# Weight operands prepared for fast multiplications: stores one operand behind, raw quarters two ahead, plain quarters not stored

## The chip, the core and the metric

The kernel runs on one core of a Trainium2 chip. Its time is the device time of one execution in microseconds. TensorE (PE) multiplies, ScalarE (ACT), VectorE (DVE) and GpSimd (POOL) work on rows, SyncE (SP) issues the DMAs spoken of here. Every engine runs its own instructions in order.

## The reference

One layer of an encoder, 1024 tokens of width 1024, in float32:

```
h   = rms_norm(x);  lru_in, gate, q, k, v, g_r, g_a = split(h @ W_in)
y_r = (gelu(gate) * rg_lru(conv4(lru_in))) @ W_lru_o
y_a = diff_attention(rms_norm(q), rms_norm(k), v) @ W_attn_o
x   = x + (sigmoid(g_r) * y_r + sigmoid(g_a) * y_a) @ W_out
x   = x + memory_cross_attention(rms_norm(x), rms_norm(mem))
x   = x + experts(rms_norm(x))        # 32 experts, two per token
```

The change is about the three products with W_attn_o (`w_ao`), W_lru_o (`w_lo`) and W_out (`w_out`).

## The kernel before

Every float32 operand is split in two parts: `h`, a rounded copy made by ScalarE, and `l`, the rest, made by VectorE (`split`, L323 to L325; for weights that stream in, L97 and L101). A product is three matmuls, hh, hl and lh (`mm3`, L158 to L161). All big tiles are slots of 128 x 1024 of one pool with 51 of them; a tile that is allocated waits until the last reader of the slot it gets is done, a DMA included.

The stages, in the profiled execution's time:

- 0 to 86 us: x is loaded, normed and transposed.
- to 357 us: the projections v (first half), q and k (four units, `qk_steps`), v (second half). One unit has four quarters, `pqk<unit>_<quarter>` or `pv<unit>_<quarter>`, each 48 matmuls into a two-bank tile of which there are two. After a quarter ScalarE empties its bank twice: `sq` (L350, squares) and `tm` (L351, a copy); then VectorE sums (L353), GpSimd forms the root (L224, L225), VectorE scales `tm` (L356), and GpSimd rotates a part of it (L361 to L364). TensorE transposes `tm` into `pT<unit>_<quarter>_<i>` (L374), ScalarE evicts that to `qk` (L375).
- Between the matmuls of this stage `prepare` (L438) works for later: each of the three products above is done with 7 instead of 8 block multiplications (1024 x 1024 in quarters, sums and differences of quarters being the operands). For each weight and each half `lp` it loads four raw quarters `qw_*` (L431), forms the seven operands with additions on VectorE (L411), splits each into `phw_*` on ScalarE and `plw_*` on VectorE, and stores both in DRAM, in `pre_d` (L454, L455). The raw quarters of the next weight half are loaded when operand 5 is emitted. `tm_proj` advances it by `PRE[0]` steps after each half quarter.
- 357 to 870 us: attention and gates; to 966 us: the recurrence.
- 966.70 to 1197 us: the three fast multiplications (`multiply`), 21 products `g` of 10.9 us, seven for each weight: w_ao first, w_lo from g = 7 at 1043, w_out from g = 14 at 1119.13 us. `preloaded` loads the stored operands back two products ahead, `computed` forms and splits those of the activations (`op<n><p><lp>h`, `l`, L914 to L924) one product ahead.
- to 1300 us: attention to the memory and the router; to 1964 us: the experts, whose weights stream in by DMA.

The order of the instructions on an engine comes from a list scheduler in the compiler, which places them by priority and by its own estimate of times; the code's order is the priority. Loads of `prepare` and `preloaded` carry an extra dependence on the last matmul that the code had issued (`W.after(d, W.last)`), the stores none.

Of the kernel before, what the change touches and what calls it, by code (L numbers as in the profile page):

```python
# [12 lines left out]
F32R = mybir.dt.float32r  # L13
BF = mybir.dt.bfloat16
I32 = mybir.dt.int32
AF = mybir.ActivationFunctionType
OP = mybir.AluOpType
# [27 lines left out]
class Weights:  # L45
# [20 lines left out]
    def load(self):  # L66
        while self.loaded < min(len(self.pieces), self.split + self.load_ahead):
            i = self.loaded
            t = self.pool.tile([P, 1024], F32, tag="s", name=f"wraw{i}")
            src = self.pieces[i]  # L70
            j = min(i - self.load_ahead, self.split - 1)
            if len(src.shape) == 2:
                todo = [(t, src)]
            else:
                to = t.rearrange("p (k h c) -> p k h c", k=2, h=2)
                todo = [(to[:, k], src[k]) for k in range(2)]
            for to, src in todo:
                d = self.nc.sync.dma_start(to, src)
                if j >= 0:
                    self.after(d, self.h_ins[j])  # L80
                if self.floor is not None:
                    self.after(d, self.floor)
            self.dma.append(d)
            if self.flying and i >= self.flying:
                self.after(d, self.dma[i - self.flying], sync=True)
            self.raw[i] = t
            self.loaded += 1
# [44 lines left out]
def block_kernel(ctx, tc, a):  # L132
    nc = tc.nc
# [10 lines left out]
    V, A, G, E = nc.vector, nc.scalar, nc.gpsimd, nc.tensor  # L144

    def slot(name, dt=F32, shape=(P, 1024)):
        return S.tile(list(shape), dt, tag="s", name=name)

    def bank(name, dt=F32, shape=(P, 512)):
        return pb1.tile(list(shape), dt, tag="b1", name=name)  # L150

    def bank2(name, dt=F32, shape=(P, 1024)):
        return pb2.tile(list(shape), dt, tag="b2", name=name)

    def f(x):
        return x.bitcast(F32)
# [37 lines left out]
    W = Weights(nc, tc, S, pieces)  # L194
# [3 lines left out]
    for tb in range(NB):  # L198
        t = slot(f"x{tb}")
# [76 lines left out]
    for i in range(8):  # L276
        G.memset(frq[:, i:i + 1], INV_FREQ[i])
    V.tensor_tensor(ang, posf[:, :, None].to_broadcast([P, NB, 8]), frq[:, None, :].to_broadcast([P, NB, 8]),
                    op=OP.mult)
# [43 lines left out]
    def split(src, h, l):  # L323
        A.activation(h, src, AF.Copy)  # L324
        V.tensor_tensor(l, src, f(h), op=OP.subtract)  # L325
# [99 lines left out]
    def half(t, i, lp):  # L425
        return t[4 * (i // 2) + 2 * lp:4 * (i // 2) + 2 * lp + 2, :, (i % 2) * 512:(i % 2) * 512 + 512].rearrange(
            "h p c -> p h c")

    def quarter(name, src):
        t = slot(name)  # L430
        d = nc.sync.dma_start(t.rearrange("p (h c) -> p h c", h=2) if len(src.shape) == 3 else t, src)  # L431
        if W.last is not None:
            W.after(d, W.last)
        return t

    pre_d = {n: dp.tile([7, 2, 2, P, 1024], F32, name=f"pre_{n}") for n in ("w_ao", "w_lo", "w_out")}

    def prepare():  # L438

        units = [(n, lp) for n in pre_d for lp in range(2)]  # L440

        def load(n, lp):
            return {i: [quarter(f"q{n}{lp}{i}", a[n][i % 2, 2 * (i // 2) + lp] if n == "w_out" else half(a[n], i, lp))]
                    for i in range(4)}

        q = load(*units[0])
        yield
        for u, (n, lp) in enumerate(units):
            nxt = []

            def emit(p, tiles):
                h, l = slot(f"ph{n}{lp}{p}", F32R), slot(f"pl{n}{lp}{p}", F32R)
                split(tiles[0], h, l)
                nc.sync.dma_start(pre_d[n][p, lp, 0], f(h))  # L454
                nc.sync.dma_start(pre_d[n][p, lp, 1], f(l))  # L455
                if p == 5 and u + 1 < len(units):
                    nxt.append(load(*units[u + 1]))

            yield from operand_steps(q, n == "w_out", emit)
            q = nxt[0] if nxt else None  # L460

    pre = prepare()
    W.split_ahead = 4
    first = v_steps(0)
# [432 lines left out]
    stages, ops = [], {}  # L897
    QUARTER = {1: 0, 4: 2, 5: 3, 6: 1}

    def preloaded(name):  # L900
        while True:
            for p in range(7):
                r = []
                for lp in range(2):
                    t = [slot(f"{name}{p}{lp}{x}", F32R) for x in "hl"]
                    for i in range(2):
                        d = nc.sync.dma_start(f(t[i]), pre_d[name][p, lp, i])
                        W.after(d, W.last)
                    r.append(t)
                yield r  # L910

    def computed(q, moving, scale=None):
        done = []

        def emit(p, tiles):
            r = []
            for lp, t in enumerate(tiles):
                h, l = slot(f"op{len(ops)}{p}{lp}h", F32R), slot(f"op{len(ops)}{p}{lp}l", F32R)
                if scale is None:
                    W.after(A.activation(h, t, AF.Copy), W.last)  # L920
                    V.tensor_tensor(l, t, f(h), op=OP.subtract)
                else:
                    W.after(A.activation(h, t, AF.Copy, scale=scale), W.last)
                    V.scalar_tensor_tensor(l, t, scale, f(h), op0=OP.mult, op1=OP.subtract)  # L924
                r.append((h, l))
            done.append(r)

        steps = operand_steps(q, moving, emit)
        for _ in range(7):
            while not done:  # L930
                next(steps)
            yield done.pop()

    def lane_out(t, blk, k):
        return [x[:, (blk % 2) * 512 + k * P:(blk % 2) * 512 + k * P + P] for x in t[blk // 2]]
# [4 lines left out]
    def operands(g, side):  # L940
        if g // 7 < len(stages):
            ops[g, side] = next(stages[g // 7][side])

    def multiply(n, before, out):
        lane = stages[n][2]
        p1, u2, u3 = [None] * 2, [None] * 2, [None] * 2
        for p in range(7):
            g = 7 * n + p
            ta, tb_ = ops.pop((g, 0)), ops.pop((g, 1))
            for blk in range(4):  # L950
                lp, c = blk // 2, slice((blk % 2) * 512, (blk % 2) * 512 + 512)
                if g % 2 == 0:
                    if blk % 2 == 0:
                        both = bank2(f"pw{n}_{p}_{blk}")
                    ps = both[:, c]
                else:
                    ps = bank(f"pw{n}_{p}_{blk}")
                for k in range(4):
                    rh, rl = (x[:, (k % 2) * 512:(k % 2) * 512 + 512] for x in tb_[k // 2])
                    mm3(ps, *lane(ta, blk, k), rh, rl, k == 0, k == 3)  # L960
                if blk == 0:
                    if p < 6:
                        before(p + 1)
                    for d, kind in ((1, "computed"), (2, "preloaded")):
                        for side in range(2):
                            if (g + d) // 7 < len(stages) and stages[(g + d) // 7][side].__name__ == kind:
                                operands(g + d, side)
                if p in (0, 2, 3) and blk % 2 == 0:
                    (p1 if p == 0 else u2 if p == 2 else u3)[lp] = slot(f"u{n}_{p}_{lp}")
                if g % 2 == 0:  # L970
                    if blk % 2 == 0:
                        continue
                    ps, c = both, slice(0, 1024)
                if p == 0:
                    A.activation(p1[lp][:, c], ps, AF.Copy)
                elif p in (2, 3):
                    to, x = (u2, p1) if p == 2 else (u3, u2)
                    V.tensor_tensor(to[lp][:, c], x[lp][:, c], ps, op=OP.add)
                else:
                    out(p, blk, ps, {1: p1, 4: u3, 5: u3, 6: u2}[p][lp], c)  # L980
                if p == 5:
                    V.tensor_tensor(u2[lp][:, c], u2[lp][:, c], ps, op=OP.add)
                if blk % 2 == 1:
                    if p == 2:
                        p1[lp] = None
                    elif p == 5:
                        u3[lp] = None
                    elif p == 6:
                        u2[lp] = None
            del ta, tb_  # L990
# [379 lines left out]
    def x1_add(p, blk, ps, prev, c):  # L1370
# [10 lines left out]
        if p >= 5:  # L1381
            W.tick(1)

    multiply(2, x1_load, x1_add)
    W.split_ahead = 2

# [10 lines left out]
    for op in SEQ.split():  # L1397
        kind, n = op[0], int(op[1])
# [147 lines left out]
    x = [ex_prep("0", xe)]  # L1546
# [139 lines left out]
```

## Time and profile before

| what | us |
|---|---|
| median of three runs (lowest, highest) | 1965.78 (1963.65, 1971.49) |
| the profiled execution | 1976.86 |
| its span | 1975.0 |
| TensorE busy in the span | 1854.7 (94%) |
| VectorE busy | 1442.8 (73%) |
| ScalarE busy | 1145.0 (58%) |
| GpSimd busy | 354.5 (18%) |
| DMA, mean over the span | 224 GB/s |
| start of the first fast multiplication | 966.70 |
| start of its products 15 and 16 | 1130.01, 1140.89 |

The shares are means over stages that have different limits. In the projection stage TensorE has idle gaps and the granted clock falls below 1.00; from 350 us to the end of the multiplications it has few; in the expert stage the DMA engines are busy nearly all the time (348 GB/s in 1500 to 1700 us). A change in one stage is read from the rows of that stage.

### The profile page before, as it was taken

The numbers are of one execution on the slowest core, as the hardware profiler recorded it, in microseconds if no ns is written. First come the engines' busy times: TensorE is split into PE (matmuls) and PEld (weight loads), VectorE is DVE, ScalarE is ACT, GpSimd is POOL, SyncE is SP. The second block draws the span as 40 slices with busy tenths as digits, with TensorE's granted clock in tenths as the row PEclk, the third lists the DMA queues.
The fourth block names the chain that finished last, engine by engine and source line by source line (L and its number), as shares of the span: only waits on it lengthen the run. The fifth ranks groups of instructions, "written<-read, shape, count | busy, mean of one in ns | idle before, by whom it ended". The sixth has DMA issues, their size and how long they took to land.

```text
span 1975.0 us, 26124 instructions
## 1 busy us (share of the span) xinstructions
PE 1854.7 (94%) x9070; PEld 1470.1 (74%) x9070; DVE 1442.8 (73%) x1918; ACT 1145.0 (58%) x1667; POOL 354.5 (18%) x432
## 2 busy tenths in 40 slices
PE   6997889999999999979999999996999999999996
PEld 5876767888888888867888887885777777777664
DVE  5364554467677775887876976776899999999885
ACT  5243444455556554776722225542888888888775
POOL 2143543012212221111000001211111111111110
PEclk9998989999999999989999999997999999999998
DMA  5476978543433313122787842167999999999996
GB/s 197 171 271 250 332 268 323 143 123 107 129 107 107 107 54 121 35 80 78 297 290 246 298 157 71 54 261 286 319 340 345 334 362 350 346 339 350 343 341 212
DMA packets 144341, 441.50 MB, mean 224 GB/s; under 512 B 17552, under 2 KB 30992, under 8 KB 144208
## 3 DMA queue, kind: packets, MB, share of 16 engines
q1 hardware_dynamic: 132304, 410.20, 58.4%
q0 software_dynamic: 7296, 17.04, 3.8%
q10 hardware_dynamic: 4608, 12.58, 1.6%
q8 instruction: 72, 1.18, 0.2%
q14 instruction: 61, 0.50, 0.1%
HBM read 355.86 MB, written 92.27 MB: 227 GB/s over the span
## 4 chain that ended last, share of the span: by engine, by line
PE 40%; issue 17%; DMA 15%; DVE 7%; ACT 4%; POOL 1%; POOLq 0%; ACTq 0%; SPq 0%; DVEq 0%
DMA out<-y,idx 13%; PE pw L159 4%; PE pw L160 4%; PE pw L161 4%; PE pga L159 3%; PE pga L160 3%; PE pga L161 3%; PE pS L557 1%; PE pS L558 1%; DVE st L562 1%; PE pw L599 1%; PE pcq L160 1%; PE pco L160 1%; PE pco L159 1%; PE pcq L161 1%
## 5 line engine op out<-in xcount | busy, mean ns | idle before, releaser
L101 DVE TENSOR_TENSOR wl<-wraw,wh 128x1024 fp32r<-128x1024 f32 x456 | 547.7, 1225 | 120.5 <-ACT wh L97 110.0
L97 ACT ACTIVATE wh<-wraw 128x1024 fp32r<-128x1024 f32 x456 | 472.4, 1057 | 78.7 <-DMA wraw<-in_w_dn 17.7
L160 PE MATMUL pgu<-wl,xeh 128*96 128x512 f32 x512 | 203.6, 398 | 1.3 <-DVE wl L101 1.2
L159 PE MATMUL pgu<-wh,xeh 128*96 128x512 f32 x512 | 203.5, 397 | 0.0
L161 PE MATMUL pgu<-wh,xel 128*96 128x512 f32 x512 | 200.9, 392 | 0.0
L569 ACT ACTIVATE p<-pS,st 128x256 f32<-128x256 f32 (+7 forms) x128 | 94.9, 747 | 102.7 <-DVE st L562 53.0
L159 PE MATMUL pqk<-wh,hH 128*128 128x512 f32 x256 | 105.1, 411 | 29.1 <-ACT tm L351 29.1
L159 PE MATMUL pga<-hH,wh 128*128 128x512 f32 x320 | 127.5, 398 | 2.5 <-DVE wT L603 2.5
L160 PE MATMUL pga<-hL,wh 128*128 128x512 f32 x320 | 126.0, 394 | 0.0
L161 PE MATMUL pga<-hH,wl 128*128 128x512 f32 x320 | 125.5, 392 | 0.0
L160 PEld LDWEIGHTS pgu<-wl,xeh 128*96 128x96 f32 x512 | 82.8, 162 | 44.6 <-DVE wl L101 13.9
L1515 POOL DMA_INDIRECT out<-y,idx x32 | 46.4, 1451 | 366.3 <-ACT y L1514 361.4
L578 POOL TENSOR_SCALAR p<-p,st 128x128 f32<-128x128 f32 (+3 forms) x64 | 55.0, 859 | 301.1 <-DVE st L577 166.1
L159 PEld LDWEIGHTS pgu<-wh,xeh 128*96 128x96 f32 x512 | 82.8, 162 | 33.3 <-ACT xeh L324 0.2
L161 PEld LDWEIGHTS pgu<-wh,xel 128*96 128x96 f32 x512 | 82.8, 162 | 33.2 <-DVE xel L325 0.2
L160 PE MATMUL py<-wl,ah 128*96 128x512 f32 x256 | 102.8, 402 | 2.4 <-DVE wl L101 2.2
L160 PE MATMUL pqk<-wl,hH 128*128 128x512 f32 x256 | 103.4, 404 | 0.0
L161 PE MATMUL pqk<-wh,hL 128*128 128x512 f32 x256 | 103.2, 403 | 0.0
L161 PE MATMUL py<-wh,ah 128*96 128x512 f32 x256 | 100.4, 392 | 0.0
L159 PE MATMUL py<-wh,ah 128*96 128x512 f32 x256 | 80.5, 394 | 3.3 <-ACT wh L97 3.2
L159 PEld LDWEIGHTS pqk<-wh,hH 128*128 128x128 f32 x256 | 50.4, 197 | 41.6 <-ACT tm L351 31.3
L557 PE MATMUL pS<-kH,qS 128*128 128x512 f32 (+2 forms) x192 | 69.5, 366 | 4.9 <-ACT p L569 4.9
(1025 smaller groups left out, 4599.6 us busy)
## 6 DMA issues: line engine op xcount, KB each, us to landing
wraw<-in_w_gu SPq DMA_DIRECT2D x256, 512.0 KB, 6.4
wraw<-in_w_dn SPq DMA_DIRECT2D x128, 512.0 KB, 6.7
wraw<-in_w_cm SPq DMA_DIRECT2D x32, 512.0 KB, 4.6
x<-in_x SPq DMA_DIRECT2D x16, 512.0 KB, 6.5
wraw<-in_w_qk SPq DMA_DIRECT2D x32, 256.0 KB, 5.5
qk_d<-qk SPq DMA_DIRECT2D x32, 256.0 KB, 5.9
qr<-qk_d SPq DMA_DIRECT2D x32, 256.0 KB, 5.0
kr<-qk_d SPq DMA_DIRECT2D x32, 256.0 KB, 5.5
```

The source lines that it names most:

```text
L97: ins = nc.scalar.activation(h, raw, AF.Copy)
L101: nc.vector.tensor_sub(l, raw, h.bitcast(F32))
L159: W.seen(E.matmul(out, lh, rh, start=start, stop=False))
L160: E.matmul(out, lh, rl, start=False, stop=False)
L161: E.matmul(out, ll, rh, start=False, stop=stop)
L557: E.matmul(ps[:, o:o + c], lhs, kh_[h, m][:, o:o + c], start=True, stop=False)
L558: E.matmul(ps[:, o:o + c], lhs, kl_[h, m][:, o:o + c], start=False, stop=True)
L562: V.reduce_max(mx[:, m:m + 1], ps[:, :n], axis=AX.X, negate=True)
L569: A.activation(p[:, :n], ps[:, :n], AF.Exp, bias=mx[:, m:m + 1], accum_out=ls[:, m:m + 1])
L578: G.tensor_scalar(pp[1][:, :n], pp[1][:, :n], rl[:, 1:2], 0.0, op0=OP.mult, op1=OP.add)
L599: E.transpose(ps[:, j, i * P:(i + 1) * P], w[:, kb * P:(kb + 1) * P], ident)
L1515: G.indirect_dma_start(out=a["out"][:, :], out_offset=bass.IndirectOffsetOnAxis(ap=dest, axis=0), in_=y, in_offset=None, bounds_check=T - ...
```

## The change

- `prepare` issues the two stores of an operand when the next one is emitted (`late`, `store`), now with the extra dependence on the last matmul, and loads the four raw quarters of the next weight half at operand 3 instead of 5.
- Three of the seven operands of w_lo and of w_out are a quarter of the weight itself, without any addition (`PLAIN`: operand to quarter). These are neither split nor stored in `prepare`: 12 operands, 12 instructions on ScalarE and 12 on VectorE, 24 stores of 512 KB. In `preloaded` their raw quarter is loaded (one load instead of two), and `split_plain` splits it, one product ahead.

```diff
--- before.py
+++ after.py
@@ -433,31 +433,45 @@
             W.after(d, W.last)
         return t
 
+    PLAIN = {"w_ao": {}, "w_lo": {0: 0, 1: 1, 4: 3}, "w_out": {0: 0, 1: 2, 6: 3}}
     pre_d = {n: dp.tile([7, 2, 2, P, 1024], F32, name=f"pre_{n}") for n in ("w_ao", "w_lo", "w_out")}
 
+    def weight_quarter(n, i, lp):
+        return quarter(f"q{n}{lp}{i}", a[n][i % 2, 2 * (i // 2) + lp] if n == "w_out" else half(a[n], i, lp))
+
     def prepare():
 
         units = [(n, lp) for n in pre_d for lp in range(2)]
 
         def load(n, lp):
-            return {i: [quarter(f"q{n}{lp}{i}", a[n][i % 2, 2 * (i // 2) + lp] if n == "w_out" else half(a[n], i, lp))]
-                    for i in range(4)}
+            return {i: [weight_quarter(n, i, lp)] for i in range(4)}
 
         q = load(*units[0])
         yield
+        late = []
+
+        def store():
+            while late:
+                n, p, lp, hl = late.pop()
+                for i in range(2):
+                    W.after(nc.sync.dma_start(pre_d[n][p, lp, i], f(hl[i])), W.last)
+
         for u, (n, lp) in enumerate(units):
             nxt = []
 
             def emit(p, tiles):
+                store()
+                if p == 3 and u + 1 < len(units):
+                    nxt.append(load(*units[u + 1]))
+                if p in PLAIN[n]:
+                    return
                 h, l = slot(f"ph{n}{lp}{p}", F32R), slot(f"pl{n}{lp}{p}", F32R)
                 split(tiles[0], h, l)
-                nc.sync.dma_start(pre_d[n][p, lp, 0], f(h))
-                nc.sync.dma_start(pre_d[n][p, lp, 1], f(l))
-                if p == 5 and u + 1 < len(units):
-                    nxt.append(load(*units[u + 1]))
+                late.append((n, p, lp, (h, l)))
 
             yield from operand_steps(q, n == "w_out", emit)
             q = nxt[0] if nxt else None
+        store()
 
     pre = prepare()
     W.split_ahead = 4
@@ -902,6 +916,9 @@
             for p in range(7):
                 r = []
                 for lp in range(2):
+                    if p in PLAIN[name]:
+                        r.append(weight_quarter(name, PLAIN[name][p], lp))
+                        continue
                     t = [slot(f"{name}{p}{lp}{x}", F32R) for x in "hl"]
                     for i in range(2):
                         d = nc.sync.dma_start(f(t[i]), pre_d[name][p, lp, i])
@@ -930,6 +947,15 @@
             while not done:
                 next(steps)
             yield done.pop()
+
+    def split_plain(g, side):
+        r = ops[g, side]
+        if not isinstance(r[0], list):
+            for lp in range(2):
+                t = [slot(f"pl{g}{lp}{x}", F32R) for x in "hl"]
+                W.after(A.activation(t[0], r[lp], AF.Copy), W.last)
+                V.tensor_tensor(t[1], r[lp], f(t[0]), op=OP.subtract)
+                r[lp] = t
 
     def lane_out(t, blk, k):
         return [x[:, (blk % 2) * 512 + k * P:(blk % 2) * 512 + k * P + P] for x in t[blk // 2]]
@@ -965,6 +991,8 @@
                         for side in range(2):
                             if (g + d) // 7 < len(stages) and stages[(g + d) // 7][side].__name__ == kind:
                                 operands(g + d, side)
+                            elif d == 1 and g + 1 < 21 and stages[(g + d) // 7][side].__name__ == "preloaded":
+                                split_plain(g + 1, side)
                 if p in (0, 2, 3) and blk % 2 == 0:
                     (p1 if p == 0 else u2 if p == 2 else u3)[lp] = slot(f"u{n}_{p}_{lp}")
                 if g % 2 == 0:
```

Three places of the changed order. In the projection stage, ScalarE, between the first two quarters of qk unit 1: `wh` is a weight copy of the stream, `phw_ao16` the copy of the last operand of w_ao, `phw_lo00` that of w_lo's operand 0, `sq1_1` and `tm1_1` empty the bank of quarter 1. Before:

```order
L97 ACTIVATE wh15_1250<-wraw15_1135 128x1024
L324 ACTIVATE phw_ao16_1257<-qw_ao11_933 128x1024
L324 ACTIVATE phw_lo00_1263<-qw_lo00_1218 128x1024
L350 ACTIVATE sq1_1_1270<-pqk1_1_1174 128x1024
L351 ACTIVATE tm1_1_1269<-pqk1_1_1174 128x1024
L324 ACTIVATE phw_lo01_1325<-qw_lo01_1220 128x1024
```

And now:

```order
L97 ACTIVATE wh15_1248<-wraw15_1133 128x1024
L324 ACTIVATE phw_ao16_1257<-qw_ao11_891 128x1024
L350 ACTIVATE sq1_1_1264<-pqk1_1_1180 128x1024
L351 ACTIVATE tm1_1_1263<-pqk1_1_1180 128x1024
L350 ACTIVATE sq1_2_1347<-pqk1_2_1294 128x1024
```

The copy of operand 0 of w_lo no longer stands ahead of `sq1_1`, and that of operand 1 no longer behind `tm1_1`.

TensorE at the end of the stage, where qk unit 3 goes over into the second v unit: `pT3_1` and `pT3_2` are the transposes of quarters 1 and 2 of qk unit 3, `pv1_0` and `pv1_1` the first two quarters of v. Before:

```order
L160 MATMUL pv1_0_2328<-wl23_2086,hH7_150 128x512
L374 MATMUL pT3_2_0_2222<-ident_100,tm3_2_2205 128x128 x4
L374 MATMUL pT3_2_1_2228<-ident_100,tm3_2_2205 128x128 x4
L161 MATMUL pv1_0_2328<-wh23_2085,hL7_158 128x512
L159 MATMUL pv1_1_2411<-wh20_1942,hH0_143 128x512
```

And now:

```order
L159 MATMUL pv1_0_2260<-wh20_1894,hH0_143 128x512
L160 MATMUL pv1_0_2260<-wl20_1895,hH0_143 128x512
L161 MATMUL pv1_0_2260<-wh20_1894,hL0_151 128x512
L374 MATMUL pT3_1_0_2072<-ident_100,tm3_1_2057 128x128 x4
L374 MATMUL pT3_1_1_2078<-ident_100,tm3_1_2057 128x128 x4
L374 MATMUL pT3_2_0_2156<-ident_100,tm3_2_2139 128x128 x4
L374 MATMUL pT3_2_1_2162<-ident_100,tm3_2_2139 128x128 x4
L159 MATMUL pv1_0_2260<-wh20_1894,hH1_144 128x512
```

The transposes of quarter 2 stood before the last matmul of `pv1_0`, and those of quarter 1 three matmuls before the end of `pqk3_3`; now both stand behind the third matmul of `pv1_0`.

VectorE in the third multiplication, at its third product (g = 16): `op120l` and `op121l` are the lower parts of its two activation operands, `tg` the activations that are added up for operands, `x1` the residual, `pw2_1` the results of the product before. Before:

```order
L924 SCALAR_TENSOR_TENSOR op120l_9443<-tg0_00_8255,op120h_9442 128x1024
L1375 TENSOR_TENSOR x1_4_9358<-x1_4_9358,pw2_1_0_9423 128x512
L411 TENSOR_TENSOR tg0_21_8485<-tg0_21_8485,tg0_01_8257 128x1024
L924 SCALAR_TENSOR_TENSOR op121l_9447<-tg0_01_8257,op121h_9446 128x1024
L411 TENSOR_TENSOR tg0_00_8255<-tg0_30_8561,tg0_00_8255 128x1024
```

And now:

```order
L941 SCALAR_TENSOR_TENSOR op120l_9391<-tg0_00_8183,op120h_9390 128x1024
L1403 TENSOR_TENSOR x1_4_9298<-x1_4_9298,pw2_1_0_9371 128x512
L411 TENSOR_TENSOR tg0_01_8185<-tg0_11_8567,tg0_01_8185 128x1024
L1403 TENSOR_TENSOR x1_5_9300<-x1_5_9300,pw2_1_1_9408 128x512
L1403 TENSOR_TENSOR x1_6_9302<-x1_6_9302,pw2_1_2_9423 128x512
L411 TENSOR_TENSOR tg0_00_8183<-tg0_30_8489,tg0_00_8183 128x1024
L411 TENSOR_TENSOR tg0_21_8413<-tg0_21_8413,tg0_01_8185 128x1024
L1403 TENSOR_TENSOR x1_7_9304<-x1_7_9304,pw2_1_3_9438 128x512
L941 SCALAR_TENSOR_TENSOR op121l_9395<-tg0_01_8185,op121h_9394 128x1024
```

Two rows stood between `op120l` and `op121l`; now there are seven. Ahead of these, the subtractions `pl150l` and `pl151l` of the plain operand of g = 15 have come in, between `op111l` and the additions to `x1`, and `pl140l` and `pl141l` of g = 14 behind `op101l`.

## Rows read from the trace of the kernel before

**Rows 1.** One stretch each: length, busy us of every engine, TensorE clock, DMA share, GB/s
```profile
150.00:200.00 50.00, 36.94 (x163) 30.24 (x162) 24.63 (x21) 20.88 (x25) 17.51 (x19) 0.86 0.70 259
...
350.00:400.00 50.00, 50.00 (x239) 41.87 (x238) 26.59 (x48) 23.02 (x46) 4.71 (x12) 1.00 0.43 128
1043.00:1119.00 76.00, 76.00 (x337) 62.94 (x336) 54.62 (x52) 17.02 (x19) 0.61 (x4) 1.00 0.77 266
1119.00:1141.00 22.00, 22.00 (x99) 18.22 (x98) 21.32 (x26) 5.53 (x6) 0.00 (x0) 1.00 0.69 240
```

**Rows 2.** Waits of 90 to 360 us: engine, line, waited for, us in total, times, longest
```profile
PE pqk L159 <- ACT tm L351: 29.1, 6, 13.1
...
PE pT L374 <- POOL tm L364: 2.3, 2, 1.9
```

**Rows 3.** TensorE timeline: start, us, line, tiles, [idle before and its releaser]
```profile
134.82 0.79 PE L159 MATMUL pqk<-wh,hH 128*128 128x512 f32 x1 [4.00 <-ACT tm L351]
...
173.34 0.79 PE L159 MATMUL pqk<-wh,hH 128*128 128x512 f32 x1 [13.06 <-ACT tm L351]
173.93 0.63 PE L160 MATMUL pqk<-wl,hH 128*128 128x512 f32 x1
...
230.69 0.80 PE L159 MATMUL pqk<-wh,hH 128*128 128x512 f32 x1 [5.58 <-ACT tm L351]
...
258.06 0.50 PE L159 MATMUL pqk<-wh,hH 128*128 128x512 f32 x1 [2.01 <-ACT tm L351]
258.40 0.40 PE L160 MATMUL pqk<-wl,hH 128*128 128x512 f32 x1
...
277.03 1.09 PE L374 MATMUL pT<-ident,tm 128*128 128x128 f32 x8 [1.90 <-POOL tm L364]
...
289.18 0.79 PE L159 MATMUL pqk<-wh,hH 128*128 128x512 f32 x1 [3.10 <-ACT tm L351]
...
320.26 0.80 PE L159 MATMUL pv<-wh,hH 128*128 128x512 f32 x1 [4.40 <-ACT tm L351]
```

**Rows 4.** ScalarE timeline, 163 to 179 us
```profile
163.50 1.05 ACT L324 ACTIVATE phw_ao<-qw_ao 128x1024 fp32r<-128x1024 f32 x1
170.41 1.06 ACT L324 ACTIVATE phw_lo<-qw_lo 128x1024 fp32r<-128x1024 f32 x1 [5.86 <-DMA qw_lo<-in_w_lo]
171.37 1.00 ACT L350 ACTIVATE sq<-pqk 128x1024 f32<-128x1024 f32 x1
...
178.82 1.03 ACT L351 ACTIVATE tm<-pqk 128x1024 f32<-128x1024 f32 x1 [3.67 <-DMA pre_w_ao<-phw_ao]
```

**Rows 5.** SyncE's queue, 163 to 170 us
```profile
163.57 0.96 SPq L431 DMA_DIRECT2D qw_lo<-in_w_lo  x1
...
165.88 3.47 SPq L431 DMA_DIRECT2D qw_lo<-in_w_lo  x3
```

**Rows 6.** GpSimd and VectorE timelines, 272 to 275 us
```profile
272.81 0.45 POOL L361 TENSOR_TENSOR sq<-tm,ropeS 128x128 f32<-128x128 f32 x1
273.23 1.43 POOL L362 TENSOR_TENSOR sq<-tm,ropeS 128x128 f32<-128x128 f32 x1
...
272.87 1.47 DVE L356 TENSOR_TENSOR tm<-tm,rq_0r 128x1024 f32<-128x1024 f32 x1 [2.80 <-POOL rq_0r L225]
```

**Rows 7.** DMAs of 60 to 360 us: count, KB each, median us to landing
```profile
pre_w_ao<-phw_ao SPq DMA_DIRECT2D x14, 512.0 KB, 2.9
...
qw_lo<-in_w_lo SPq DMA_DIRECT2D x8, 512.0 KB, 7.9
```

**Rows 8.** VectorE timeline, 1119 to 1138 us
```profile
1119.33 0.69 DVE L1034 TENSOR_TENSOR u<-u,pw 128x512 f32<-128x512 f32 x1 [0.71 <-PE pw L161]
...
1126.23 1.22 DVE L924 SCALAR_TENSOR_TENSOR op111l<-tg,op111h 128x1024 fp32r<-128x1024 f32 x1
...
1136.48 1.22 DVE L924 SCALAR_TENSOR_TENSOR op121l<-tg,op121h 128x1024 fp32r<-128x1024 f32 x1
```

**Rows 9.** TensorE timeline, 1140 to 1142 us
```profile
1140.89 0.39 PE L159 MATMUL pw<-w_out20h,op120h 128*128 128x512 f32 x1
```

## The prediction

> **What bounds the kernel now.** I read the stretches first, then the waits, then the timelines of the engines that end those waits. In the table of stretches [rows 1] the reader is to compare TensorE's busy column with the length. From 350 us on, and through the three fast multiplications (966 to 1197 us), TensorE is busy all the time at granted clock 1.00; only the projection stage, where `prepare` runs, is not: 36.94 us of 50 in its worst stretch, with a granted clock of 0.86. So a cheaper `prepare` can pay there and almost nowhere else, and what is moved into the multiplications is paid in a place where TensorE has no idle time to hide it in, but VectorE has: 54.62 us busy of 76, except from 1119 to 1141 us, where it is busy 21.32 of 22.
>
> The waits of the projection stage [rows 2] say who is late: 29.1 us of TensorE's idle time end on `tm` of ScalarE (L351, the second of two copies that empty a `pqk` bank), 2.3 us on GpSimd's L364. The timeline of TensorE [rows 3] gives each: 4.00, 13.06, 5.58, 2.01, 3.10, 4.40 us, and 1.90 us at the transposes; 29.1 less the five of `pqk` leaves 1.4 us for the sixth, near 213 us. After most of them come matmuls of 0.63 us, the clock's level of 1.2 GHz, where full speed shows 0.40. In the timeline 8, 14, 7, 14 and 14 matmuls follow the stalls of 134, 173, 230, 289 and 320 us at that level; starts lie 0.43 us apart instead of 0.23, so 57 x 0.20 = 11.4 us. With the 2.3 us idle at the transposes and the 4.40 at 320, the stage loses 29.1 + 2.3 + 4.4 + 11.4 = about 47 us. It is ScalarE's queue that does this: it is not full (20.88 us of 50), but in order, and a split of `prepare` or a copy that waits stands ahead of the `tm` that TensorE needs.
>
> **The change, part by part.** The profiled execution took 1976.86 us (span 1975.0), the median of the runs is 1965.78. I take differences from the trace and set them against the median; the 11 us between them is an uncertainty, since some of the profiled stalls may be shorter in ordinary runs.
>
> *Splits that leave the stage.* Twelve copies on ScalarE (1.06 us each [rows 4]) and twelve subtractions on VectorE (1.22 us each, as the like one in [rows 8]) go: 12.7 and 14.6 us of engine time, worth only what stood ahead of a `tm`. By stall, in the changed order:
> - 134 us: ScalarE's order there is the same. It stays; I allow 0.6 us loss.
> - 173 us: ScalarE ends a `phw_ao` at 164.55, then waits 5.86 us for the raw quarter of the first `phw_lo` [rows 4]; SyncE issued one load at 163.57 and the other three only from 165.88, behind stores that wait for their splits [rows 5]. In the changed kernel operand 0 of w_lo is plain, the row is gone and `sq`, `tm` follow: 164.5 + 0.9 + 1.0 gives TensorE free at 166.5 instead of 173.34. But that `tm` takes a slot that a store must first have left. A store lands in 2.9 us by the median of its group, the raw loads take 7.9 [rows 7], and `tm` at 178.82 waited 3.67 us for such a store [rows 4]. Bounds: 6.8 us gained with no wait, 2.8 with 4 us of it. I take 5.3, TensorE free near 168, nearer to the median.
> - 213 us: two splits ahead of `tm` are gone, 1.4 gained.
> - 230 us: the transposes of pT2_0 stand after 32 matmuls of pqk2_2 instead of 48, 16 x 0.23 = 3.6 us earlier, and the evictions, splits and `tm` behind them too. 5.58 falls to about 2.2; with the shorter idle the seven slow matmuls (1.4) may go: 4.9 gained.
> - 258 us: two splits, 1.9 us by ScalarE's spacing of 0.95, leave the queue ahead of `tm`: 2.01 falls to 0 to 0.6, 1.7 gained.
> - 277 us: the two groups of transposes are now apart, so GpSimd has to feed one at a time: 2.3 falls to about 1, 1.3 gained.
> - 289 us: pT3_0 stands nine matmuls later (2 us), one split less (0.95): 1.4 lost after rounding up.
> - 320 us: pT3_1 and pT3_2 stand together behind three matmuls of pv1_0, as the order shows, so the evictions no longer come at the end of pv1_0, right before the `tm` that is needed. 4.40 goes, and 14 x 0.20 = 2.8 with it: 7.2 gained.
>
> Sum: -0.6 + 5.3 + 1.4 + 4.9 + 1.7 + 1.3 - 1.4 + 7.2 = 19.8 us.
>
> *What is late next.* Four groups of transposes now stand closer behind their GpSimd chains (at about 230, 239, 264 and 287 us on the new time). Each can cost between 0 and 1.9 us, the wait seen at 277 us [rows 3]; I take 0.5 each, 2 us. The row of GpSimd that varies most is L362: 1.43 us where VectorE's L356 runs beside it (272.87 to 274.34), 0.45 for the same shape just before [rows 6].
>
> The Trainium skill (SBUF — State Buffer, section Who interferes with whom) says that a VectorE instruction with two inputs in SBUF contends with a GpSimd instruction that reads SBUF. The trace agrees with 1.43 beside 0.45 us. By that rule the denser VectorE work between the remaining stalls could lengthen each of the four chains by 1 us, 4 us instead of 2, while twelve two-input subtractions fewer speak the other way; the sum holds without it.
>
> *Stores one operand later, loads two operands earlier.* 24 stores of 512 KB go, 12.6 MB. The others are issued by SyncE with the next operand. By this a `ph`/`pl` pair holds its two slots for one operand longer, and the earlier loads hold four slots sooner. I cost this at nothing: the plain operands leave two slots each free, and the loads no longer stand behind a split that is not yet done (the 2.3 us between 163.57 and 165.88). If the cover is gone it is a slot wait like the 3.67 us [rows 4], once per unit at worst, five units, 18 us: the bound above.
>
> *What comes into the multiplications.* Twelve copies on ScalarE (17.02 us busy of 76 there: hidden) and twelve subtractions on VectorE of 1.22 us. Their loads fall from 24 to 12, and the DMA share is 0.77 and 0.69 [rows 1]: no cost. At most of the twelve VectorE has room: 21.4 us idle over the seven products of w_lo, 3 us each, for 2.4. The two before 1119 us push the following rows by 2.3 us; 0.71 us idle at 1119.33 [rows 8] takes up part. In the changed order I put the second split of w_out's operand 1 at 1129.2, needed at 1130.0, and op121l, which ended at 1137.7, at 1144.2: two splits (2.3), 0.7 of slack less, and four rows that now stand ahead of it. TensorE begins that product at 1140.89 [rows 9], and in the changed order needs op121l at its fifteenth matmul, 14 x 0.23 later, 1144.1. Cost 0 to 2 us there, and 0 to 2 at the end, where the last two splits delay the rows that the transposes of 1197 us wait for. A loss down to zero is excluded nowhere, a gain is (nothing waits there now). I take 0.8.
>
> Sum: 19.8 - 2 - 0.8 = 17 us. What follows the stage (attention, LRU, experts) waits for TensorE's place in its order and moves with it: 1965.78 - 17 = 1949.
>
> **Rivals.** *The gaps are made again.* ScalarE still runs in order, and the evictions in its queue wait for transposes; if a GpSimd chain or a late transpose holds each shortened stall, only the gain at 173 us (2.8 to 6.8) and the 1.4 at 213 remain. For: all stalls but two end on the same `tm`. Against: at 230, 258 and 320 us the instructions that preceded it are gone or earlier. 1965.78 - 6 = 1960.
>
> *Slower: slots.* A store issued one operand later keeps its pair, and four raw quarters come two operands early, while the pool has 51 slots for everything. Whenever a `tm`, `sq` or `qk` tile is next in the ring, ScalarE waits for a landing. Price 3.67 us a unit for five units, and the clock's fall behind three of these stalls at 2.8 us: 27 us; less the 17 gained, 10 slower: 1976. It decides if more than four of the units show such a wait. For: that wait exists already at 178.82. Against: there are 24 stores fewer, and the slots of twelve pairs.
>
> *Not what it says.* If the profiled stalls are longer than those in ordinary runs (the 11 us), the stage gives back less: 1965.78 - 8.5 = 1957 at half the gain. Against: the stalls follow from the written order of the queues, and the clock fell behind them, which no chance of one execution makes.
>
> **Numbers.** Chances: the forecast 0.56 (its own range 1940 to 1957), made again 0.20, half the gain 0.12, slower 0.12. The bound for a difference that can be told from none is 0.5%, 9.8 us: below 1956.0 faster, above 1975.6 slower. Faster: nine tenths of the forecast's 0.56, half of the 0.12, a quarter of the 0.20, 0.62 in all. Slower: 0.6 of the 0.12 and a little of the rest, 0.09. The same: 0.29. Range: the low end takes every stall at its best (173 us 1.5 more, chains 2, multiplications 0.8, 134 and 289 us unchanged 2) and the other 36 slow matmuls at full clock (7.2): 13.5 less, 1936; the high end reaches through the gaps made again and half way to the slower case: 1971.
>
> **What would show it.** Right: no ScalarE wait for a raw quarter of w_lo ahead of a `tm` near 165 us and TensorE's stall there at 6 to 9 us; none at 320 us; the first multiplication starting about 18 us earlier than at 966.7; TensorE busy all through 1110 to 1145 us. Wrong: `tm` or `sq` waiting for landings of stores in several units, waits of transposes on L364 of more than 1 us each, a gap before the products of w_out, or an unchanged start of the attention.

## The result, and the profile after

The changed kernel takes 1946.67 us (median of five runs, 1945.81 to 1952.38) against 1965.78 before: 19.1 us less, ratio 0.9907 (95% interval 0.9886 to 0.9929). Forecast were 1949 and 17 us less. Its profiled span is 1944.9 us.

The stretches after, with the columns of [rows 1]; the multiplications now stand 22.0 us earlier (the first starts at 944.68), so 1020 to 1096 and 1096 to 1118 are, to within 1 us, the same work as 1043 to 1119 and 1119 to 1141 before:

```profile
150.00:200.00 50.00, 43.38 (x193) 35.63 (x193) 28.19 (x24) 22.15 (x27) 26.12 (x21) 0.93 0.69 251
300.00:350.00 50.00, 50.00 (x230) 41.61 (x230) 15.36 (x21) 16.80 (x28) 7.45 (x9) 1.00 0.71 230
1020.00:1096.00 76.00, 76.00 (x337) 62.90 (x337) 60.24 (x58) 22.41 (x25) 0.66 (x4) 1.00 0.69 230
1096.00:1118.00 22.00, 22.00 (x99) 18.22 (x98) 22.00 (x29) 4.97 (x5) 0.00 (x0) 1.00 0.69 262
```

The projection stage's worst stretch has 43.38 us of TensorE instead of 36.94, and 300 to 350 us is full. VectorE, which took the twelve subtractions of the multiplications, is busy 60.24 us of 76 instead of 54.62 and then all 22.00 of 22; TensorE does not notice.

TensorE's remaining stalls, in its timeline with the columns of [rows 3]; these four are all that exceed 0.8 us between 90 and 345 us (17.9 us in all, 35.4 before):

```profile
136.09 0.80 PE L159 MATMUL pqk<-wh,hH 128*128 128x512 f32 x1 [4.64 <-ACT tm L351]
...
168.19 0.80 PE L159 MATMUL pqk<-wh,hH 128*128 128x512 f32 x1 [6.62 <-ACT tm L351]
...
219.87 0.50 PE L159 MATMUL pqk<-wh,hH 128*128 128x512 f32 x1 [1.95 <-ACT tm L351]
...
221.30 0.63 PE L161 MATMUL pqk<-wh,hL 128*128 128x512 f32 x1
...
274.26 0.80 PE L159 MATMUL pqk<-wh,hH 128*128 128x512 f32 x1 [4.68 <-ACT tm L351]
```

The row of 221.30 shows what stands behind such a stall: matmuls of 0.63 us, as before. The stall near 168 is the one that was 13.06 us long. ScalarE's queue at that place, which answers [rows 4]:

```profile
160.32 1.27 ACT L375 ACTIVATE qk<-pT,gq 128x512 f32<-128x512 f32 x2 [9.70 <-PE pT L374]
161.48 1.05 ACT L97 ACTIVATE wh<-wraw 128x1024 fp32r<-128x1024 f32 x1
162.43 2.00 ACT L324 ACTIVATE phw_ao<-qw_ao 128x1024 fp32r<-128x1024 f32 x2
164.32 1.05 ACT L97 ACTIVATE wh<-wraw 128x1024 fp32r<-128x1024 f32 x1
165.27 1.05 ACT L324 ACTIVATE phw_ao<-qw_ao 128x1024 fp32r<-128x1024 f32 x1
166.21 1.01 ACT L350 ACTIVATE sq<-pqk 128x1024 f32<-128x1024 f32 x1
167.12 1.02 ACT L351 ACTIVATE tm<-pqk 128x1024 f32<-128x1024 f32 x1
```

No row between the eviction and `tm` waits any more: the eviction of a transpose, two weight copies, three copies of `prepare`, `sq` and `tm`, end to end. TensorE starts with the end of `tm`. What is left of the stall is ScalarE's work between the transposes and `tm`, less the four matmuls that TensorE still had to do behind them.

The stall of 5.58 us near 230 became the 1.95 us at 219.87, and there no copy has left the queue. ScalarE before, and then in the changed kernel:

```profile
225.86 2.00 ACT L97 ACTIVATE wh<-wraw 128x1024 fp32r<-128x1024 f32 x2
227.75 1.05 ACT L324 ACTIVATE phw_lo<-qw_lo 128x1024 fp32r<-128x1024 f32 x1
```

```profile
215.04 2.01 ACT L97 ACTIVATE wh<-wraw 128x1024 fp32r<-128x1024 f32 x2
216.94 1.06 ACT L324 ACTIVATE phw_lo<-qw_lo 128x1024 fp32r<-128x1024 f32 x1
```

What differs is the order on TensorE: the transposes ahead of these copies stand 16 matmuls before the end of their quarter, where none was left before. The stall of 4.40 us near 320 is gone in the same way, with two copies of `prepare` behind the transposes in both kernels. These two make 8.0 of the 17.5 us of idle time that are gone.

VectorE in the third multiplication, answering [rows 8], and TensorE there:

```profile
1102.28 1.22 DVE L941 SCALAR_TENSOR_TENSOR op111l<-tg,op111h 128x1024 fp32r<-128x1024 f32 x1
...
1104.55 1.21 DVE L957 TENSOR_TENSOR pl150l<-qw_out,pl150h 128x1024 fp32r<-128x1024 f32 x1
1105.69 1.22 DVE L957 TENSOR_TENSOR pl151l<-qw_out,pl151h 128x1024 fp32r<-128x1024 f32 x1
...
1120.71 1.21 DVE L941 SCALAR_TENSOR_TENSOR op121l<-tg,op121h 128x1024 fp32r<-128x1024 f32 x1
```

```profile
1121.59 0.39 PE L159 MATMUL pw<-w_out21h,op121h 128*128 128x512 f32 x1
...
1122.49 0.39 PE L161 MATMUL pw<-w_out21h,op121l 128*128 128x512 f32 x1
```

`op121l` ends at 1121.92; the first matmul that reads it (L161) starts at 1122.49. That is a margin of 0.57 us, and no gap of TensorE exceeds 0.1 us in the three multiplications.

### The profile page after: what moved, and what is told of

It is laid out like the page before. It is cut to its first block, busy times and chain, and to the rows that moved or that the text cites. A ratio compares the mean times of both kernels' runs of the same rounds, so it can differ in the third digit from the quotient of the medians.

```text
span 1944.9 us, 26026 instructions
## 1 busy us (share of the span) xinstructions
PE 1843.9 (95%) x9070; PEld 1466.4 (75%) x9070; DVE 1441.8 (74%) x1918; ACT 1145.2 (59%) x1667; POOL 349.5 (18%) x432
## 4 chain that ended last, share of the span: by engine, by line
PE 50%; issue 18%; DMA 15%; DVE 7%; ACT 6%; POOL 2%; SPq 0%; POOLq 0%; ACTq 0%; DVEq 0%
DMA out<-y,idx 13%; PE pw L161 4%; PE pw L160 4%; PE pw L159 4%; PE pga L159 3%; PE pga L160 3%; PE pga L161 3%; PE pqk L159 2%; PE pqk L160 2%; PE pqk L161 2%; PE pv L159 2%; PE pv L160 2%; PE pv L161 1%; PE pS L571 1%; PE pS L572 1%
## 5 line engine op out<-in xcount | busy, mean ns | idle before, releaser
L97 ACT ACTIVATE wh<-wraw 128x1024 fp32r<-128x1024 f32 x456 | 471.8, 1057 | 67.6 <-PE pgu L161 16.9
L161 PE MATMUL pgu<-wh,xel 128*96 128x512 f32 x512 | 201.1, 393 | 0.0
L161 PE MATMUL pga<-hH,wl 128*128 128x512 f32 x320 | 125.5, 392 | 0.0
L161 PEld LDWEIGHTS pgu<-wh,xel 128*96 128x96 f32 x512 | 82.9, 162 | 33.3 <-DVE xel L325 0.2
L161 PE MATMUL pqk<-wh,hL 128*128 128x512 f32 x256 | 102.9, 402 | 0.0
L161 PE MATMUL py<-wh,ah 128*96 128x512 f32 x256 | 100.5, 392 | 0.0
L375 ACT ACTIVATE qk<-pT,gq 128x512 f32<-128x512 f32 x32 | 20.2, 686 | 106.2 <-PE pT L374 100.4
```

Of the source, the lines that this page charges most:

```text
L97: ins = nc.scalar.activation(h, raw, AF.Copy)
L161: E.matmul(out, ll, rh, start=False, stop=stop)
L375: A.activation(out[i][:, :, c], pt, AF.Copy, scale=gq[:, i:i + 1])
```

## Experiments

Where the projections end tells the kernels apart: what follows, up to the multiplications, takes about 610 us in each of them (609.7 to 610.7). Columns: the start of the last matmul of v, TensorE's idle time, and the measured ratio.

| kernel | last matmul of v, us | idle of TensorE over 0.8 us in 90 to 345 us | ratio to before (95%) |
|---|---|---|---|
| before | 356.4 | 35.4 | 1 |
| before, second profile (e4) | 352.4 | 34.5 | |
| changed | 334.9 | 17.9 | 0.9907 (0.9886 to 0.9929) |
| no plain operands (e1) | 353.6 | 32.8 | 0.9994 (0.9980 to 1.0007) |
| plain operands alone (e2) | 336.1 | 19.8 | 0.9914 (0.9891 to 0.9936) |
| multiplications alone (e3) | 352.7 | 35.0 | 0.9999 (0.9984 to 1.0015) |
| split, not stored (e5) | 349.5 | 30.3 | 0.9977 (0.9963 to 0.9991) |
| before, tm first (e6) | 322.2 | 10.8 | 0.9839 (0.9816 to 0.9862) |
| changed, tm first (e7) | 310.2 | 3.3 | 0.9781 (0.9766 to 0.9796) |
| before, early pT2_0 (e8) | 354.0 | 34.8 | |

Measured from the second profile of the kernel before (e4), the projections of the changed kernel, e2, e5, e6 and e7 end 17.5, 16.3, 2.9, 30.2 and 42.2 us earlier. By their ratios these kernels take 18.3, 16.9, 4.5, 31.7 and 43.1 us less. So the gains are made in the projections, within 2 us.

**e1, no plain operands**: late stores and early loads alone.

```diff
-    PLAIN = {"w_ao": {}, "w_lo": {0: 0, 1: 1, 4: 3}, "w_out": {0: 0, 1: 2, 6: 3}}
+    PLAIN = {"w_ao": {}, "w_lo": {}, "w_out": {}}
```

> Stores one operand late and raw quarters two operands early, but all seven operands of every weight half are still split and stored in the projection stage. Theory A (the gain is the twelve splits that leave ScalarE's queue ahead of tm): only the wait for w_lo's first raw quarter goes, 3 to 6 us less than before, 1960 to 1963 us, with stalls near 230, 289 and 320 us still there. Rival B (the gain is SyncE's queue: stores out of the way, loads earlier): at least 15 us less, at most 1951 us. Rival C (late stores hold slots): no gain or slower, 1966 us and above.

Measured: 1968.92 against 1968.88 us, no difference. By the number this is rival C's range; rival B is refuted, and of theory A's 3 to 6 us nothing is left. TensorE's longer stalls, and two pieces of ScalarE's queue:

```profile
169.48 0.80 PE L159 MATMUL pqk<-wh,hH 128*128 128x512 f32 x1 [7.63 <-ACT tm L351]
...
228.35 0.80 PE L159 MATMUL pqk<-wh,hH 128*128 128x512 f32 x1 [5.58 <-ACT tm L351]
...
259.67 0.80 PE L159 MATMUL pqk<-wh,hH 128*128 128x512 f32 x1 [5.11 <-ACT tm L351]
...
293.29 0.79 PE L159 MATMUL pqk<-wh,hH 128*128 128x512 f32 x1 [7.72 <-ACT tm L351]
```

```profile
166.47 1.05 ACT L324 ACTIVATE phw_lo<-qw_lo 128x1024 fp32r<-128x1024 f32 x1
...
288.89 1.02 ACT L350 ACTIVATE sq<-pqk 128x1024 f32<-128x1024 f32 x1 [1.41 <-DVE plw_out L325]
292.22 1.02 ACT L351 ACTIVATE tm<-pqk 128x1024 f32<-128x1024 f32 x1 [2.30 <-DMA pre_w_out<-phw_out]
```

The earlier loads did what they were for: `phw_lo` at 166.47 has its raw quarter, and that stall is 7.63 us, where the two profiles of before have 13.06 and 13.22. But the transposes stand elsewhere in this order. Those of pT2_2 have two matmuls of their quarter left, not 16, and 2.01 became 5.11 near 260. The stall near 320, which theory A expected to stay, is 0.74 us, with 17 matmuls left instead of one. Near 293 `tm` waits 2.30 us for a late store of `phw_out`, and that stall is 7.72 us. What was gained was given back.

Rival C's mechanism is there too: in 90 to 345 us ScalarE waits eight times for the landing of a late store, 13.9 us in all, where the kernel before has two such waits of 4.0 us and the changed kernel one of 2.85. Only the one near 293 stands right before a stall of TensorE.

**e2, plain operands alone**: stores at once, next load at operand 5, as before.

```diff
             def emit(p, tiles):
-                store()
-                if p == 3 and u + 1 < len(units):
-                    nxt.append(load(*units[u + 1]))
                 if p in PLAIN[n]:
                     return
...
-                late.append((n, p, lp, (h, l)))
+                nc.sync.dma_start(pre_d[n][p, lp, 0], f(h))
+                nc.sync.dma_start(pre_d[n][p, lp, 1], f(l))
+                if p == 5 and u + 1 < len(units):
+                    nxt.append(load(*units[u + 1]))
```

> The plain operands leave the projection stage and are split in the multiplications, but stores are issued at once and raw quarters loaded at operand 5, as before. Theory A: 15 to 20 us less than before, 1946 to 1951 us. Rival B: less than 6 us gained, 1960 us and above.

Measured: 0.9914, the whole effect (the median of 1953.40 belongs to a chip on which before took 1968.88). Two of its stalls:

```profile
222.20 0.79 PE L159 MATMUL pqk<-wh,hH 128*128 128x512 f32 x1 [3.98 <-ACT tm L351]
...
276.74 0.80 PE L159 MATMUL pqk<-wh,hH 128*128 128x512 f32 x1 [4.56 <-ACT tm L351]
```

With pT2_0 seven matmuls before the end of its quarter the stall that was 5.58 is 3.98: 7 x 0.227 = 1.6 less. In the changed kernel it has 16 left, and 1.95 remain, 3.6 less.

**e3, multiplications alone**: e2's times of stores and loads (those lines are left out of the cut), and all operands still split and stored in `prepare` (the three plain ones for nobody).

```diff
-                if p in PLAIN[n]:
-                    return
```

> Projection stage as before (all operands split and stored, stores at once, loads at operand 5); only the multiplications load raw quarters of the plain operands and split them there, so this is the price of what is added. Theory A: 0 to 2 us slower than before, 1966 to 1968 us, with no gap of TensorE before the products of w_out. Rival D (VectorE, full from 1119 to 1141 us, lets TensorE wait for splits): 4 us or more slower, 1970 us and above, with gaps there.

Measured: 0.9999, that is 3 us either way at the most, and no gap of TensorE over 0.11 us in the multiplications. What the change adds there costs nothing that can be told.

**e4, before again.**

> The kernel before once more, for a second profile. If the 11 us by which its first profiled execution lay above the median belong to the experts' stage, this one takes about 1966 us, its projections end within 1 us of 356.6 us and its expert matmuls last about 559 us instead of 568. If they belong to the projections' stalls, these end 5 to 10 us earlier.

Measured: 1969.66 us. The projections end 4 us earlier than in the first profile, the experts' matmuls last 566.1 us from first to last (567.8). Neither of the two readings holds alone. In the other profiles that stretch lasted 559.1 (changed) to 568.6 us (e1), with 561.5 in e8 and 568.5 in e6. It goes with no part of the change, and what moves it stays open. Two waits of the first profile were its own: at the transposes near 277 us TensorE waits 0.39 us here instead of 2.3, and near 289 us 4.20 instead of 3.10 (4.73 in e3, whose projections are the same).

**e5, split but not stored**: the plain operands are split in `prepare` and the results dropped.

```diff
-                if p in PLAIN[n]:
-                    return
                 h, l = slot(f"ph{n}{lp}{p}", F32R), slot(f"pl{n}{lp}{p}", F32R)
                 split(tiles[0], h, l)
-                late.append((n, p, lp, (h, l)))
+                if p not in PLAIN[n]:
+                    late.append((n, p, lp, (h, l)))
```

> The changed kernel, but the plain operands are still split in the projection stage (24 instructions whose results nobody reads); they are not stored, and the multiplications load and split the raw quarters. So the 24 stores are gone and the splits are not. Theory A (splits ahead of tm in ScalarE's queue): the stalls come back, near 230 us 5.58 (transposes after the whole quarter, three splits behind them), then 3.5 and 3.2 us; 1958 to 1968 us. Rival B (stores and DMA traffic): the gain stays, 1946 to 1953 us.

Measured: 0.9977, 4.5 us less than before: most of the gain is gone with the 24 stores still left out. The 24 instructions are the larger part, not the 12.6 MB; they also bring another order on TensorE, and e5 does not separate the two. The stalls of 5.58 and 3.50 came as worked out; the third did not, 6.03 instead of 3.2. ScalarE's queue there:

```profile
275.26 2.42 ACT L375 ACTIVATE qk<-pT,gq 128x512 f32<-128x512 f32 x4 [15.63 <-PE pT L374]
277.56 1.08 ACT L97 ACTIVATE wh<-wraw 128x1024 fp32r<-128x1024 f32 x1
278.51 2.02 ACT L324 ACTIVATE phw_out<-qw_out 128x1024 fp32r<-128x1024 f32 x2
280.40 1.07 ACT L97 ACTIVATE wh<-wraw 128x1024 fp32r<-128x1024 f32 x1
281.36 1.06 ACT L324 ACTIVATE phw_out<-qw_out 128x1024 fp32r<-128x1024 f32 x1
283.33 1.06 ACT L324 ACTIVATE phw_out<-qw_out 128x1024 fp32r<-128x1024 f32 x1 [0.92 <-DVE wl L101]
285.80 1.02 ACT L350 ACTIVATE sq<-pqk 128x1024 f32<-128x1024 f32 x1 [1.41 <-DVE plw_out L325]
286.72 1.02 ACT L351 ACTIVATE tm<-pqk 128x1024 f32<-128x1024 f32 x1
```

Here six copies in a row are more than VectorE follows, which also subtracts for each: ScalarE waits 0.92 and 1.41 us for it. That these are waits for slots that VectorE has not yet released is inferred from the tiles. My sum left VectorE out.

**e6 and e7, tm first**: in the projections of q and k the weight copies and `prepare`'s steps of a quarter are written behind its `sq` and `tm`. e6 does it to the kernel before, e7 to the changed one.

```diff
-            W.tick(1)
-            for _ in range(PRE[0]):
-                next(pre, None)
+            if not name.startswith("pqk"):
+                aside()
         return ps
+
+    def aside():
+        W.tick(1)
+        for _ in range(PRE[0]):
+            next(pre, None)
...
             A.activation(tm, ps, AF.Copy)
+            aside()
+            aside()
```

> The kernel before with one change of order: the weight copies and prepare's steps of a quarter are written behind that quarter's sq and tm instead of ahead of them; no work is left out. Theory A says a stall is 2.73 us (eviction, sq, tm) plus 0.95 for each split between the transposes and tm, less 0.227 for each matmul left in the quarter: two stalls of about 2.7 us stay (pT2_2 and pT3_0, no matmul left) of the seven, 6 to 12 us idle in all instead of 35, 1940 to 1950 us. Rival E (GpSimd's chain or the raw quarters take over as soon as ScalarE is early): idle moves to the transposes, 1955 us or more.

> The changed kernel with the same change of order. Theory A: by the same sum every stall is below 0.5 us, the 17.9 us of idle time go and the slow matmuls behind them: 18 to 24 us less than the changed kernel, 1922 to 1930 us. Rival E: waits of the transposes on GpSimd's L364 take most of it, 1940 us or more.

Measured: 0.9839 and 0.9781. e6 leaves no work out and gains more than the change: 1940.99 us against 1968.15. e7 takes 1926.74 us and beats both kernels. ScalarE in e6, and TensorE:

```profile
229.58 1.27 ACT L381 ACTIVATE qk<-pT,gq 128x512 f32<-128x512 f32 x2 [7.69 <-PE pT L380]
230.73 1.03 ACT L354 ACTIVATE sq<-pqk 128x1024 f32<-128x1024 f32 x1
231.64 1.04 ACT L355 ACTIVATE tm<-pqk 128x1024 f32<-128x1024 f32 x1
```

```profile
180.09 0.50 PE L159 MATMUL pqk<-wh,hH 128*128 128x512 f32 x1 [2.75 <-ACT tm L355]
180.43 0.40 PE L160 MATMUL pqk<-wl,hH 128*128 128x512 f32 x1
...
232.73 0.70 PE L159 MATMUL pqk<-wh,hH 128*128 128x512 f32 x1 [2.75 <-ACT tm L355]
```

Eviction, `sq`, `tm`, nothing between, and TensorE idle 2.75 us, the constant of the sum. Three such stalls came, not two (the third is 2.79 us at 260.93). In e7 three waits are left, the largest of them the transposes' on GpSimd; the third is 0.4 us:

```profile
PE pT L380 <- POOL tm L370: 1.9, 1, 1.9
...
PE pqk L159 <- ACT tm L355: 1.4, 1, 1.4
```

That is rival E at 1.9 us, and it decides nothing here. The 1.4 us at `tm` are more than the 0.5 expected; the sum gives them, 2.73 less six matmuls left. No matmul of e7's stage runs at the lower level; its granted clock is 1.00 throughout.

**e8, before with pT2_0 early**: one dependence, so that pT2_0 comes after 33 matmuls of pqk2_2.

```diff
+                if name == "pqk2_2" and j == 1 and k == 3:
+                    W.after(W.last, PT["2_0"])
```

> The kernel before with the transposes pT2_0 placed after 33 matmuls of pqk2_2 instead of 48, nothing else (the places that follow move by a few matmuls: pT2_2 has 12 left instead of 16, pT3_2 none instead of one). Theory A, by its sum: the stall near 230 us falls from 5.58 to 2.2, the one near 258 rises from 2.01 to 2.9, the one near 317 from 4.40 to 4.6. Rival F (the stall is set by when the bank or the splits' data come, not by the transposes): it stays at 5.6.

Measured (one profile):

```profile
222.61 0.33 PE L377 MATMUL pT<-ident,tm 128*128 128x128 f32 x1 [1.79 <-POOL tm L367]
...
229.28 0.50 PE L159 MATMUL pqk<-wh,hH 128*128 128x512 f32 x1 [2.14 <-ACT tm L354]
...
257.60 0.50 PE L159 MATMUL pqk<-wh,hH 128*128 128x512 f32 x1 [2.85 <-ACT tm L354]
...
258.24 0.63 PE L161 MATMUL pqk<-wh,hL 128*128 128x512 f32 x1
...
318.56 0.79 PE L159 MATMUL pv<-wh,hH 128*128 128x512 f32 x1 [4.63 <-ACT tm L354]
```

2.14, 2.85 and 4.63, where 2.2, 2.9 and 4.6 were worked out. Of the 3.4 us, 1.8 come back at once: pT2_0 now waits for GpSimd at 222.61. The last matmul of v is no earlier than in e4: the sum gives the length of a stall, and one stall shortened by order alone gained nothing here.

## Why the prediction was right

By its own steps:

- *134 us stays, 0.6 lost*: 4.64 at 136.09. Right; what lost 0.6 is the order on TensorE, with no matmul left behind the transposes instead of three.
- *173 us, TensorE free near 168*: 168.19. Right in size, partly by luck: the forecast had 1.5 us of a wait for a store in it (0 to 4), and none came, but the transposes ahead of this queue ended 1.75 us later than before (160.66 instead of 158.91), which the forecast had left out. The cause of the gain has two halves, each enough alone: without plain operands the earlier load makes 7.63 of 13.06 (e1), without earlier loads the missing row makes 6.14 (e2).
- *213, 258 and 320 us go*: no gap over 0.8 us there. Right; at 320 us by the order alone, as worked out.
- *277 us, 1.3 gained*: 1.1 us of waits at transposes are left in the stage, but the 2.3 us were the first profile's own (0.39 in e4). Against e4 nothing was gained there.
- *230 us, 2.2*: 1.95. Right, by the order alone; that its seven slow matmuls would go with it was wrong, eight follow 219.87 (1.4 us too much).
- *289 us, 1.4 lost*: 4.68 against 3.10. Right against the first profile; against e4 (4.20) 0.5 lost, and e3 has 4.73 without the change.
- *Four GpSimd chains, 2 us*: TensorE waited 1.1 us for L364 in the stage, and no longer than 0.7 at once. The rule of the Trainium skill beside this term (SBUF — State Buffer, section Who interferes with whom) would have made it 4 us by the prediction's estimate; the changed kernel shows 1.1, and the most in any run is 3.7 us (e5). The two rows read for it [rows 6] are not a clean pair, since the one of 0.45 us lies beside L356 too and began 0.06 us before it. In the same trace L361 and L362 take 0.45 to 0.46 us with no two-input VectorE instruction beside them, and 1.28 to 1.44 us in the twelve cases that begin while one runs. So the rows bear the wait out, but it hardly reached TensorE.
- *Multiplications, 0.8*: 0 within 3 us (e3). The place named was the right one, `op121l`, worked out for 1144.2 on the old time; it ended at 1121.92, and TensorE's work there had moved by 22.0, so 1143.9. It is needed two matmuls later than I had counted.
- *Stores later, loads earlier, nothing*: 0 by e1's interval (at most 4 us gained, 1.4 lost), as a gain of 5.6 (against e4) and losses of like size. The cover that the prediction named, the slots of the plain operands, shows: without them, in e1, ScalarE waits 13.9 us for landings, with them 2.85, though of the 13.9 us only 2.30 stand right before a stall. With plain operands the two parts together are also worth nothing that can be told (e2 0.9914, changed 0.9907).

One reading was too broad: TensorE is not busy all the time from 350 us on. Before, it was busy 83.44 of the 96 us from 870 to 966, at granted clock 0.93. It changes no term, since the change does nothing there.

The rival "made again" is refuted by the stalls near 213, 258 and 320 us that did not come back, "slower" by the missing landing waits (one of 2.9 us at a `sq`), "not what it says" by e4: the first profile's stage was 4 us too long, not half of the gain.

Right was the mechanism. A stall of this stage is one eviction, `sq` and `tm` (2.73 us), plus 0.95 us for each copy of a split (of `prepare` or of a weight that streams in) between the transposes and `tm`, less 0.227 us for each matmul that TensorE still has when the transposes are done. It gives 5.58 (three copies, none left), 1.95 (three, 16), 3.98 (three, 7), 4.40 (two, one left), and 2.75 (none, none left). It holds where no row of the list waits; near 173 and 289 us the waits for a raw quarter, a landing or VectorE come on top. The change takes copies out of this sum near 173, 213, 258 and 289 us and, by the order that the compiler gives the new program, puts matmuls into it near 230 and 320 us. That order was read before the run, but nothing in the change asks for it: in e1, with all splits in place, the stall at 320 us shrank and that at 258 us grew, both by the order. e6 shows what it does not touch: the splits need not be gone, they only have to stand behind `tm`.

## What to carry to other kernels

When an engine with half its time free makes another wait, list what stands in its queue between the event that it waits for and the instruction that is waited for; that list times its spacing, less the work the other engine still has, was the stall here. Move the list behind before you remove it: writing the side work after the evictions gained 1.6%, taking out twelve of its 42 operands 0.9% (with the order that came of it), both 2.2%. Work that moved into a full stage cost nothing that could be told, since the engine that took it ended before the reader, so look for the margin (0.57 us here), not for the busy share.

## What the runs showed that I had not expected

The length of a stall does not by itself say whether slow matmuls follow. 1.95 us at 219.87 in the changed kernel were followed by matmuls of 0.63 us; 2.75 us at 180.09 in e6 were not (0.40 in the next row); 2.01 us at 258 before were not [rows 3], 2.85 us near the same place in e8 were (its row of 258.24). And an engine 100% busy over 22 us (VectorE, 1096 to 1118 us) held up nobody.
